# Alternating four and three seven-product pairs in the feed-forward slabs of a two-layer trunk, with the feed-forward cut into four groups

## The chip, the cores and the metric

The kernel runs on one core of a Trainium2 chip. Its engines work from queues of their own, each in order: TensorE (PE) multiplies matrices, VectorE (DVE) and ScalarE (ACT) work element by element, GpSimd (POOL) does little here, SyncE (SP) issues transfers. The metric is the time of one execution in microseconds on the device, median of several runs.

## What is computed

The reference is a trunk of two layers on 256 tokens of width 2048, in float32. The change lies in the second half of a layer:

```python
x = x + mix @ w_out[l]
h = _rmsnorm(x, norm2_g[l])
x = x + (jax.nn.silu(h @ ffn_w_gate[l]) * (h @ ffn_w_up[l])) @ ffn_w_down[l]
```

The hidden width D_FF is 5632, which is 44 blocks of 128 columns. The width 2048 is 16 chunks of 128. Ahead of this stand the input projection, eight retention heads and a gated recurrence; a final norm follows the second layer.

## The kernel before, in words

All weights come from memory in float32 and are split on the core into two parts, `whi` (ScalarE rounds a copy) and `wlo` (VectorE subtracts that copy from the weight), and every activation likewise into a pair (`op`). A product then takes three matmuls: high by high, high by low, low by high (L616 to L618). The down projection and the other projections with weights as the stationary side do the same with two matmuls a block, one of 512 and one of 256 columns (L233, L236).

The feed-forward of a layer is worked in groups (THIRDS), each of several slabs and then a down phase. A **slab** is four blocks of the hidden width (SLAB), gate and up together, for both halves of the tokens; a layer has 11 slabs, the groups of before 4, 4 and 3. A slab runs through the 16 chunks in eight pairs, one **unit** each. There are two kinds of unit:

- A plain unit (P) makes eight block products, 24 matmuls. Its weights (1 MB) are prepared in two halves of 1024 columns: two `whi` and two `wlo`.
- A unit with seven products (F, `p < FAST`) forms sums and differences of blocks first, a Strassen-like scheme with 21 matmuls. Its weights are prepared in four steps (`gate_parts`, `up_parts`, `first_sums`, `second_sums`): three halves of 1024, one of 512, and three extra subtractions on VectorE in the raw buffer (L649, L654, L655). The `whi` of `first_sums` needs the result of L655. The matching sums of the activations are made once a layer by `combined`, in the output projection, and stay for all slabs.

The order of a slab's units is F P F P F P P P. After the last F `shared` takes four sums out of PSUM (L705 to L710); at the slab's end `gate` and `up` (L714 to L721) combine the rest, `columns` transposes the result on TensorE (L731), and `operands_of` makes pairs of it (L143, L144). These pieces are issued some ticks later, among the next unit's blocks: a tick is one block of a unit.

After the slabs of a group come 16 units of the **down phase**, one for each chunk of the output, each over the group's 16 or 12 blocks of the hidden width, and each ends with `residual` (L462, L463), which adds the PSUM result to x. `hold` moves the last blocks of the first units behind one another, so that the last slab's operands have time to become ready.

Three raw buffers (RAW) take the weights; the load of unit n + 3 is issued after the last preparation of unit n. Six tiles each of `whi` and `wlo` (HALVES) hold prepared halves: ahead of every block `prepare` issues up to two preparations, as long as the half six places back has been used. The pairs of activations share 32 tiles (`ops`).

Of the kernel before, what the change touches and what calls it, by code (L numbers as in the profile page):

```python
# [11 lines left out]
F32 = mybir.dt.float32  # L12
F32R = mybir.dt.float32r
# [10 lines left out]
NL = 8  # L24
CHUNK = 64
EPS = 1e-6
THIRDS = [(0, 16), (16, 16), (32, 12)]
SLAB = 4
FAST = 3
RAW = 3  # L30
HALVES = 6
WARM = 12
# [56 lines left out]
def trunk(ctx: ExitStack, tc, a, out):  # L89
# [375 lines left out]
    def after_residual(k, nxt, gains):  # L465

        accumulate("xa", X[:, k, :], k == 0)
        st[nxt, k] = pair(X[:, k, :], gains(k))
        if k == KD - 1:
            tk.after(2, lambda: sums([st["xa"]], D, "rs"))  # L470
            if nxt == "h1":
                tk.after(4, lambda: rows("rs"))
        if nxt == "h2" and k % 2 and k < 2 * FAST:
            tk.after(3, lambda: combined(k // 2, gains))

    def combined(p, gains):

        r = one_p.tile([P, 4, T], F32, tag="rot4", name="asum")
        for i in range(2):
            S.activation(out=r[:, i, :], in_=X[:, 2 * p + i, :], func=AF.Copy, scale=gains(2 * p + i))  # L480
        a11, a21, a12, a22 = (r[:, i, j * P : (j + 1) * P] for i in range(2) for j in range(2))
        f = r[:, 2:4, :].rearrange("p a (b t) -> p (a b) t", b=2)
        V.tensor_tensor(out=f[:, 0, :], in0=a21, in1=a22, op=ALU.add)
        V.tensor_tensor(out=f[:, 1, :], in0=f[:, 0, :], in1=a11, op=ALU.subtract)
        V.tensor_tensor(out=f[:, 2, :], in0=a11, in1=a21, op=ALU.subtract)
        V.tensor_tensor(out=f[:, 3, :], in0=a12, in1=f[:, 1, :], op=ALU.subtract)
        if p == 0:
            st["s01"] = one_p.tile([P, 2, 4, 2, P], F32R, tag="v", name="s01")
        if p == 2:
            st["s2"] = one_p.tile([P, 4, 2, P], F32R, tag="gy0", name="s2")  # L490
        t = st["s2"] if p == 2 else st["s01"][:, p]
        S.activation(out=t[:, :, 0, :], in_=f, func=AF.Copy)
        V.tensor_tensor(out=t[:, :, 1, :], in0=f, in1=t[:, :, 0, :].bitcast(F32), op=ALU.subtract)
        st["sums", p] = t

    def rotation():
        r = one_p.tile([P, 2, T], F32, tag="rotl", name="rotl")
# [48 lines left out]
    def layer_units(l):  # L546
        res = v_units(l)
        res[0].begin = lambda: tk.after(30, rotation)
        proj = lambda n, done, begin=None: column_unit(
            a["w_in"][l, n], KD, lambda k: st["h1", k], done, begin)  # L550
        heads = []
        for h in range(NH):
            q_done, k_done, g_done = head(l, h)
            heads += [proj(h, q_done), proj(8 + h, k_done), proj(16 + h, g_done)]
        heads[-4], heads[-3], heads[-2] = heads[-3], heads[-2], heads[-4]
        for n in range(NL):
            x_begin, x_done, y_done = lru(l, n)
            res += [proj(24 + n, x_done, x_begin), proj(32 + n, y_done)]
            for _ in range(REC_AFTER[n] if n < NL - 1 else len(heads)):
                res.append(heads.pop(0))  # L560


        order = [0, 1, 2, 3, 4, 5, 6] + list(range(8, 16)) + [7]
        for n in range(KD):
            def done(ps, n=n):
                residual(n, ps)
                after_residual(n, "h2", lambda k: col("g2", l * KD + k))
            res.append(column_unit(a["w_out"][l, n], KD, lambda k: st["mix", l, k], done, order=order))
        hold(res[-KD : -KD + 2])


        for t, (f0, nf) in enumerate(THIRDS):
            for f in range(f0, f0 + nf, SLAB):
                res += slab_units(l, f, f == f0)
            res[-1].done = columns_again
            first = len(res)
            for n in range(KD):
                def done(ps, n=n, t=t):
                    residual(n, ps)
                    if t == len(THIRDS) - 1:  # L580
                        if l + 1 < DEPTH:
                            after_residual(n, "h1", lambda k: col("g1", (l + 1) * KD + k))
                        else:
                            last(n)
                res.append(column_unit(a[f"w_down{t}"][l, n], nf, lambda k, f0=f0: st["act", f0 + k], done))
            hold(res[first : first + (2 if nf == 16 else 3)])
        return res


    def slab_units(l, f0, first):  # L590
# [3 lines left out]

        c = {}
        res = []

        def start():
            if first:
# [32 lines left out]
        def piece(t, k):  # L632
            return t.rearrange("p (f k w) -> p f k w", f=SLAB, k=2)[:, :, k, :]

        turns = [q for p in range(FAST) for q in (p, FAST + p)] + list(range(2 * FAST, KD // 2))
        for p in turns:
            u = Unit(loader(p))
            plain = p >= FAST
            if not plain:
                def gate_parts(u=u):  # L640
                    hi, lo = half_tiles(u, 0)
                    parts(hi, lo, u.raw[:, 0:1024])

                def up_parts(u=u):
                    hi, lo = half_tiles(u, 1)
                    flat = lambda t: t[:, 0:512].rearrange("p (f w) -> p f w", f=SLAB)
                    parts(flat(hi), flat(lo), piece(u.raw[:, 1024:2048], 1))
                    r = u.raw.rearrange("p (c f k w) -> p c f k w", c=2, f=SLAB, k=2)
                    V.tensor_tensor(out=r[:, :, :, 0, :], in0=r[:, 1].rearrange("p f k w -> p k f w"),  # L649
                                    in1=r[:, :, :, 0, :], op=ALU.subtract)  # L650

                def first_sums(u=u):
                    g, p_ = u.raw[:, 0:1024], u.raw[:, 1024:2048]
                    V.tensor_tensor(out=piece(p_, 1), in0=piece(p_, 1), in1=piece(g, 0), op=ALU.subtract)  # L654
                    V.tensor_tensor(out=piece(g, 1), in0=piece(g, 1), in1=piece(p_, 1), op=ALU.subtract)  # L655
                    hi, lo = half_tiles(u, 2)
                    parts(hi, lo, g)

                def second_sums(u=u):
                    hi, lo = half_tiles(u, 3)  # L660
                    parts(hi, lo, u.raw[:, 1024:2048])

                u.preps = [gate_parts, up_parts, first_sums, second_sums]

                def run(todo, p=p, u=u):
                    def go():
                        if p == 0 and todo[0] == 1:
                            start()
                        s = st["sums", p]
                        form = lambda i: (s[:, i, 0, :], s[:, i, 1, :])  # L670
                        x = {1: lambda: block_of(0, 2 * p), 2: lambda: block_of(0, 2 * p + 1),
                             4: lambda: block_of(1, 2 * p + 1), 3: lambda: form(3), 5: lambda: form(0),
                             6: lambda: form(1), 7: lambda: form(2)}
                        w = {1: (0, 0), 2: (0, 1), 5: (2, 0), 4: (2, 1), 7: (3, 0), 6: (3, 1)}
                        for i in todo:
                            if i == 3:
                                t = tuple(t[1][:, 0:512] for t in (u.hi, u.lo))
                            else:
                                h, k = w[i]
                                t = piece(u.hi[h], k), piece(u.lo[h], k)  # L680
                            product(i, x[i](), t, False, p == FAST - 1 and i in (1, 5, 6, 7))
                    return go

                for todo, frees in (((1, 2), [0]), ((3, 5), [1]), ((4, 7), [2]), ((6,), [3])):
                    u.add(run(todo), frees)
                if p == FAST - 1:
                    u.done = lambda: tk.after(1, shared)
            else:
                plain_halves(u, 2048)
                for j, side, i in ((0, 0, 2), (1, 0, 4), (0, 1, 3), (1, 1, 8)):  # L690
                    def go(j=j, side=side, i=i, p=p, u=u):
                        for k in range(2):
                            product(i, block_of(j, 2 * p + k), (piece(u.hi[side], k), piece(u.lo[side], k)),
                                    False, p == KD // 2 - 1 and k == 1)
                        if p == KD // 2 - 1:
                            tk.after(1, {2: lambda: gate(0), 4: lambda: gate(1), 3: lambda: up(0), 8: lambda: up(1)}[i])
                    u.add(go, [side] if j else [])
            res.append(u)
# [290 lines left out]
```

## Time and profile before

| | |
|---|---|
| median of 3 runs | 2216.33 us (2216.12 to 2218.39) |
| profiled execution | 2215.92 us, of it a span of 2214.2 us |
| TensorE clock granted over the span | 0.997 of full speed |
| busy, share of the span | PE 99%, PEld (weight load, overlaps) 84%, DVE 80%, ACT 55%, POOL 2% |
| read from memory | 418.77 MB, 190 GB/s over the span |

The median is what a changed kernel is compared with. The profiled execution is a single one, and durations come from it. Busy shares are means over stages that differ. A matmul's recorded duration is longer than the distance to the next one's start, since matmuls are pipelined; the distance is what counts.

### The profile page before, as it was taken

The numbers are of one execution on the slowest core, as the hardware profiler recorded it, in microseconds if no ns is written. First come the engines' busy times: TensorE is split into PE (matmuls) and PEld (weight loads), VectorE is DVE, ScalarE is ACT, GpSimd is POOL, SyncE is SP. The second block draws the span as 40 slices with busy tenths as digits, with TensorE's granted clock in tenths as the row PEclk, the third lists the DMA queues.
The fourth block names the chain that finished last, engine by engine and source line by source line (L and its number), as shares of the span: only waits on it lengthen the run. The fifth ranks groups of instructions, "written<-read, shape, count | busy, mean of one in ns | idle before, by whom it ended". The sixth has DMA issues, their size and how long they took to land.

```text
span 2214.2 us, 29756 instructions
## 1 busy us (share of the span) xinstructions
PE 2194.4 (99%) x11322; PEld 1861.3 (84%) x11322; DVE 1774.1 (80%) x2547; ACT 1211.5 (55%) x1620; POOL 47.5 (2%) x97
## 2 busy tenths in 40 slices
PE   9999999999999999999999999999999999999997
PEld 7888888888888888888888888888888887888886
DVE  7888887988678985888858889779886788758875
ACT  6667554655446553455646665546554455535553
POOL 0000000000000000000000000000000000000000
PEclk9999999999999999999999999999999999999998
DMA  8555454566556665555655554546665555655563
GB/s 298 182 196 186 163 182 168 190 201 230 191 169 198 198 209 198 189 178 190 212 189 192 172 201 163 179 162 199 220 209 190 172 189 190 223 186 179 173 210 113
DMA packets 224224, 422.81 MB, mean 191 GB/s; under 512 B 10192, under 2 KB 191056, under 8 KB 200016
## 3 DMA queue, kind: packets, MB, share of 16 engines
q1 hardware_dynamic: 220992, 413.96, 55.7%
q0 software_dynamic: 1792, 5.24, 0.7%
q8 instruction: 89, 1.46, 0.3%
q10 hardware_dynamic: 1296, 1.70, 0.2%
q14 instruction: 55, 0.45, 0.1%
HBM read 418.77 MB, written 2.10 MB: 190 GB/s over the span
## 4 chain that ended last, share of the span: by engine, by line
PE 62%; issue 34%; DVE 2%; ACT 1%; POOL 0%; DMA 0%; ACTq 0%; DVEq 0%; POOLq 0%
PE acc_ps L233 24%; PE acc_ps L236 12%; PE row_ps L616 6%; PE row_ps L618 6%; PE row_ps L617 6%; PE acc_ps L523 1%; PE acc_ps L525 1%; PE acc_ps L524 1%; DVE wlo L206 1%; PE sm_ps L385 1%; PE sm_ps L731 1%; ACT whi L205 0%; PE sm_ps L294 0%; DMA x<-in_x_dram 0%; POOL rc L167 0%
## 5 line engine op out<-in xcount | busy, mean ns | idle before, releaser
L205 ACT ACTIVATE whi<-raw 128x1024 fp32r<-128x1024 f32 (+2 forms) x940 | 916.7, 1003 | 837.9 <-PE acc_ps L233 440.5
L206 DVE TENSOR_TENSOR wlo<-raw,whi 128x1024 fp32r<-128x1024 f32 (+2 forms) x940 | 1063.9, 1155 | 283.4 <-ACT whi L205 277.5
L233 PE MATMUL acc_ps<-op,whi 128*128 128x512 f32 x3200 | 1014.0, 398 | 0.0
L236 PEld LDWEIGHTS acc_ps<-op,wlo 128*128 128x128 f32 x3200 | 600.7, 188 | 140.8
L236 PE MATMUL acc_ps<-op,wlo 128*128 128x256 f32 x3200 | 630.2, 278 | 0.0
L233 PEld LDWEIGHTS acc_ps<-op,whi 128*128 128x128 f32 x3200 | 490.0, 189 | 1.6
L617 PE MATMUL row_ps<-wlo,op 128*128 128x512 f32 x1078 | 420.9, 390 | 0.0
L616 PE MATMUL row_ps<-whi,op 128*128 128x512 f32 x1078 | 420.1, 390 | 0.0
L618 PE MATMUL row_ps<-whi,op 128*128 128x512 f32 x1078 | 419.9, 390 | 0.0
L616 PEld LDWEIGHTS row_ps<-whi,op 128*128 128x128 f32 x1078 | 202.3, 188 | 42.2
L618 PEld LDWEIGHTS row_ps<-whi,op 128*128 128x128 f32 x1078 | 202.4, 188 | 41.9
L617 PEld LDWEIGHTS row_ps<-wlo,op 128*128 128x128 f32 x1078 | 202.4, 188 | 41.6
L462 DVE TENSOR_TENSOR x<-acc_ps,x 128x256 f32<-128x256 f32 x128 | 54.1, 422 | 77.6 <-PE acc_ps L236 77.4
L618 PE MATMUL row_ps<-whi,s 128*128 128x512 f32 x264 | 104.8, 397 | 0.0
L617 PE MATMUL row_ps<-wlo,s 128*128 128x512 f32 x264 | 104.5, 396 | 0.0
L616 PE MATMUL row_ps<-whi,s 128*128 128x512 f32 x264 | 103.5, 392 | 0.0
L649 DVE TENSOR_TENSOR raw<-raw 128x1024 f32<-128x1024 f32 x66 | 80.3, 1216 | 0.1
L143 ACT ACTIVATE op<-sm_ps 128x256 fp32r<-128x256 f32 x88 | 33.6, 381 | 72.0 <-DVE op L144 37.3
L618 PEld LDWEIGHTS row_ps<-whi,s 128*128 128x128 f32 x264 | 50.1, 190 | 9.7
L617 PEld LDWEIGHTS row_ps<-wlo,s 128*128 128x128 f32 x264 | 49.6, 188 | 10.3
L616 PEld LDWEIGHTS row_ps<-whi,s 128*128 128x128 f32 x264 | 49.6, 188 | 10.2
L463 DVE TENSOR_TENSOR x<-acc_ps,x 128x256 f32<-128x256 f32 x128 | 54.0, 422 | 3.2
(153 smaller groups left out, 1401.8 us busy)
## 6 DMA issues: line engine op xcount, KB each, us to landing
raw<-in_w_gate_dram SPq DMA_DIRECT2D x176, 512.0 KB, 3.6
raw<-in_w_up_dram SPq DMA_DIRECT2D x176, 512.0 KB, 5.3
raw<-in_w_in_dram SPq DMA_DIRECT2D x80, 1024.0 KB, 5.0
raw<-in_w_down_dram SPq DMA_DIRECT2D x64, 1024.0 KB, 5.0
raw<-in_w_out_dram SPq DMA_DIRECT2D x32, 1024.0 KB, 4.9
raw<-in_w_down_dram SPq DMA_DIRECT2D x32, 768.0 KB, 4.2
raw<-in_w_v_dram SPq DMA_DIRECT2D x12, 1024.0 KB, 5.0
raw<-in_w_v_dram SPq DMA_DIRECT2D x16, 256.0 KB, 5.9
```

The source lines that it names most:

```text
L143: S.activation(out=t[:, 0, :], in_=x_ap, func=AF.Copy)
L205: S.activation(out=hi, in_=raw, func=AF.Copy)
L206: V.tensor_tensor(out=lo, in0=raw, in1=hi.bitcast(F32), op=ALU.subtract)
L233: PE.matmul(u.ps, lhsT=u.hi[side(k)][:, col_of(k)], rhs=operand(k).rearrange("p a t -> p (a t)"), start=k == order[0], stop=False)
L236: PE.matmul(u.ps[:, T : 2 * T], lhsT=u.lo[side(k)][:, col_of(k)], rhs=operand(k)[:, 0, :], start=False, stop=k == order[-1])
L385: PE.matmul(ps[:, j * T : (j + 1) * T], lhsT=c["w"][:, j, :], rhs=c["xc"], start=True, stop=True)
L462: V.tensor_tensor(out=X[:, k, :], in0=ps[:, T : 2 * T], in1=X[:, k, :], op=ALU.add)
L463: V.tensor_tensor(out=X[:, k, :], in0=ps[:, 0:T], in1=X[:, k, :], op=ALU.add)
L616: PE.matmul(ps, lhsT=x[0], rhs=w[0], start=go, stop=False)
L617: PE.matmul(ps, lhsT=x[0], rhs=w[1], start=False, stop=False)
L618: PE.matmul(ps, lhsT=x[1], rhs=w[0], start=False, stop=end)
L649: V.tensor_tensor(out=r[:, :, :, 0, :], in0=r[:, 1].rearrange("p f k w -> p k f w"), in1=r[:, :, :, 0, :], op=ALU.subtract)
```

## The change

Slabs with an even number within the layer have four F units, in the order F P F F P F P P; the odd ones keep three. Each of a layer's six slabs with four has 180 matmuls in place of 183. `combined` is called for a fourth pair of chunks, and its sums are held in two tiles of `ops`. So that these and the group's operands fit into the 32 tiles, the groups of the feed-forward are made smaller: three of 12 blocks (three slabs each) and one of 8 (two slabs). Each layer then has four down phases of 16 units, and `hold` takes the first three units of a group of 12 and the first four of the group of 8.

```diff
-THIRDS = [(0, 16), (16, 16), (32, 12)]
+THIRDS = [(0, 12), (12, 12), (24, 12), (36, 8)]
-FAST = 3
+FAST = (4, 3)
...
-        if nxt == "h2" and k % 2 and k < 2 * FAST:
+        if nxt == "h2" and k % 2 and k < 2 * max(FAST):
             tk.after(3, lambda: combined(k // 2, gains))
...
+        if p < 3:
+            t = st["s2"] if p == 2 else st["s01"][:, p]
+            S.activation(out=t[:, :, 0, :], in_=f, func=AF.Copy)
+            V.tensor_tensor(out=t[:, :, 1, :], in0=f, in1=t[:, :, 0, :].bitcast(F32), op=ALU.subtract)
+            st["sums", p] = [t[:, i] for i in range(4)]
+        else:
+            st["sums", p] = []
+            for i in (0, 2):
+                t = op_p.tile([P, 2, T], F32R, tag="op", name="op").rearrange("p i (a t) -> p i a t", a=2)
+                S.activation(out=t[:, :, 0, :], in_=f[:, i : i + 2, :], func=AF.Copy)
+                V.tensor_tensor(out=t[:, :, 1, :], in0=f[:, i : i + 2, :], in1=t[:, :, 0, :].bitcast(F32), op=ALU.subtract)
+                st["sums", p] += [t[:, 0], t[:, 1]]
...
-            hold(res[first : first + (2 if nf == 16 else 3)])
+            hold(res[first : first + (3 if nf == 12 else 4)])
...
+        fast = FAST[f0 // SLAB % 2]
...
-        turns = [q for p in range(FAST) for q in (p, FAST + p)] + list(range(2 * FAST, KD // 2))
+        turns = {3: (0, 3, 1, 4, 2, 5, 6, 7), 4: (0, 4, 1, 2, 5, 3, 6, 7)}[fast]
...
-            plain = p >= FAST
+            plain = p >= fast
...
-                if p == FAST - 1:
+                if p == fast - 1:
                     u.done = lambda: tk.after(1, shared)
```

## Rows read from the trace of the kernel before

**Rows 1.** The page, busy time, share and instructions of each engine.

```profile
PE 2194.4 (99%) x11322; PEld 1861.3 (84%) x11322; DVE 1774.1 (80%) x2547; ACT 1211.5 (55%) x1620; POOL 47.5 (2%) x97
```

**Rows 2.** Windows: first, middle slab; down phase; last slab; down phase.

```profile
core 0: us, PE busy (x) PEld busy (x) DVE busy (x) ACT busy (x) POOL busy (x), PEclk, DMA share, GB/s
647.70:689.30 41.60, 41.60 (x185) 34.37 (x184) 36.37 (x40) 23.36 (x26) 0.00 (x0) 1.00 0.61 198
...
731.90:774.70 42.80, 42.80 (x192) 34.93 (x192) 38.61 (x46) 24.43 (x30) 0.00 (x0) 1.00 0.60 196
...
817.50:907.60 90.10, 90.10 (x522) 78.60 (x521) 56.88 (x73) 34.83 (x36) 0.00 (x0) 1.00 0.53 178
991.80:1034.70 42.90, 42.82 (x192) 34.93 (x191) 36.12 (x44) 24.00 (x30) 0.00 (x0) 1.00 0.60 208
1034.70:1101.60 66.90, 66.90 (x387) 58.31 (x386) 54.07 (x96) 39.43 (x65) 0.00 (x0) 1.00 0.58 193
```

**Rows 3.** Timeline of VectorE over one slab; brackets: idle before, releaser.

```profile
start us, us, engine line op out<-in xcount [idle before <-releaser]
727.27 2.36 DVE L206 TENSOR_TENSOR wlo<-raw,whi 128x1024 fp32r<-128x1024 f32 x2 [1.21 <-ACT whi L205]
...
742.56 6.37 DVE L206 TENSOR_TENSOR wlo<-raw,whi 128x1024 fp32r<-128x1024 f32 x6 [1.19 <-ACT whi L205]
...
752.72 6.90 DVE L206 TENSOR_TENSOR wlo<-raw,whi 128x1024 fp32r<-128x1024 f32 x6 [1.21 <-ACT whi L205]
...
770.10 2.36 DVE L206 TENSOR_TENSOR wlo<-raw,whi 128x1024 fp32r<-128x1024 f32 x2 [1.21 <-ACT whi L205]
...
775.91 0.74 DVE L721 SCALAR_TENSOR_TENSOR cb<-cb,rc,ca 128x512 f32<-128x512 f32 x1
```

**Rows 4.** Timeline of TensorE over the same slab (durations overlap, starts count).

```profile
731.94 0.39 PE L616 MATMUL row_ps<-whi,op 128*128 128x512 f32 x1
...
733.87 0.33 PE L731 MATMUL sm_ps<-ident,cb 128*128 128x128 f32 x1
...
743.36 0.39 PE L616 MATMUL row_ps<-whi,op 128*128 128x512 f32 x1
...
745.40 0.39 PE L616 MATMUL row_ps<-whi,s 128*128 128x512 f32 x1
...
748.12 0.39 PE L616 MATMUL row_ps<-whi,op 128*128 128x512 f32 x1
...
774.74 0.39 PE L616 MATMUL row_ps<-whi,op 128*128 128x512 f32 x1
```

**Rows 5.** Timeline of VectorE across the end of a group's last slab.

```profile
1030.38 0.96 DVE L206 TENSOR_TENSOR wlo<-raw,whi 128x768 fp32r<-128x768 f32 x1 [1.76 <-ACT whi L205]
...
1042.40 0.42 DVE L144 TENSOR_TENSOR op<-sm_ps,op 128x256 fp32r<-128x256 f32 x1
```

**Rows 6.** Waits over the span: us in total, times, longest us.

```profile
ACT whi L205 <- DVE raw L655: 229.5, 66, 4.8
```

**Rows 7.** VectorE instructions by line and form: count, busy, mean ns.

```profile
L206 DVE TENSOR_TENSOR wlo<-raw,whi 128x768 fp32r<-128x768 f32 x64 | 61.1, 955 | 24.8 <-ACT whi L205 24.1
L206 DVE TENSOR_TENSOR wlo<-raw,whi 128x512 fp32r<-128x512 f32 x82 | 55.8, 683 | 0.8 <-ACT whi L205 0.7
...
L462 DVE TENSOR_TENSOR x<-acc_ps,x 128x256 f32<-128x256 f32 x128 | 54.1, 422 | 77.6 <-PE acc_ps L236 77.4
...
L144 DVE TENSOR_TENSOR op<-sm_ps,op 128x256 fp32r<-128x256 f32 x88 | 36.5, 418 | 7.5 <-ACT op L143 7.5
...
L707 DVE TENSOR_TENSOR cb<-row_ps,ca 128x512 f32<-128x512 f32 x22 | 15.0, 684 | 0.0
...
L493 DVE TENSOR_TENSOR s<-asum,s 128x512 fp32r<-128x512 f32 x6 | 4.1, 689 | 2.8 <-ACT s L492 2.8
```

**Rows 8.** The page, transfers: KB of each, median us from issue to landing.

```profile
raw<-in_w_gate_dram SPq DMA_DIRECT2D x176, 512.0 KB, 3.6
raw<-in_w_up_dram SPq DMA_DIRECT2D x176, 512.0 KB, 5.3
```

More of the change, by code (lines that the diff above doesn't have):

```diff
@@ L490, in combined @@
             st["s2"] = one_p.tile([P, 4, 2, P], F32R, tag="gy0", name="s2")
[L491 to L494, printed above, removed]
+        if p < 3:
[10 more added lines that the diff above has]
+                st["sums", p] += [t[:, 0], t[:, 1]]
     def rotation():
@@ L669, in go @@
                         s = st["sums", p]
-                        form = lambda i: (s[:, i, 0, :], s[:, i, 1, :])
+                        form = lambda i: (s[i][:, 0, :], s[i][:, 1, :])
                         x = {1: lambda: block_of(0, 2 * p), 2: lambda: block_of(0, 2 * p + 1),
@@ L680, in go @@
                                 t = piece(u.hi[h], k), piece(u.lo[h], k)
-                            product(i, x[i](), t, False, p == FAST - 1 and i in (1, 5, 6, 7))
+                            product(i, x[i](), t, False, p == fast - 1 and i in (1, 5, 6, 7))
                     return go
```

## The prediction

> **What bounds the kernel now.** I read the page first, then the windows by stage, then the timelines of VectorE and TensorE over one slab, then the waits. The page names TensorE: busy 99%, VectorE 80%, ScalarE 55% [rows 1]. A share over the whole span hides two regimes, and the windows part them. In a down phase (16 units of 16 blocks) VectorE is busy 56.88 of 90.10 us; in a slab in the middle of a group it is busy 38.61 of 42.80 [rows 2]. The timeline shows how little of the rest is free. The same instruction, the third wlo of the first F unit, starts at 727.27 and at 770.10, 42.83 us apart, and TensorE's first matmuls of the two slabs are 42.80 apart [rows 3, 4]. So both engines have the same period. In that period VectorE has three gaps of about 1.2 us, one in each F unit; each stands ahead of a wlo that waits for ScalarE's whi, which itself waits for L655, and the waits count 66 of these, one for every F unit there is [rows 3, 6]. In-order queues on both engines force that gap. What is left free is about 0.5 us a slab. TensorE sets the end, and VectorE keeps up with it with nothing to spare.
>
> **The cost of one more F unit.** From the third wlo of one F unit to the third wlo of the next, with one P between, VectorE takes 752.72 - 742.56 = 10.16 us [rows 3]. A P unit is two wlo; six in a row span 6.90 us, so they follow each other after (6.90 - 1.22) / 5 = 1.136 us, and P takes 2.27 us. F takes 10.16 - 2.27 = 7.89 us, its 1.2 us gap included. On TensorE, F runs from 743.36 to 748.12, 4.76 us for 21 matmuls, 0.227 us each [rows 4]; P has 24 of these, 5.44 us. Turning a P into an F therefore takes 0.68 us from TensorE and puts 5.62 us on VectorE.
>
> **Part 1, TensorE's saving.** FAST alternates 4, 3 over the 11 slabs of a layer, so slabs 0, 2, 4, 6, 8 and 10 get one more F: 12 in the two layers. 12 x 3 x 0.227 = 8.2 us less.
>
> **Part 2, VectorE over a slab with four.** In the period of 42.83, three F and five P make 35.0; the rest, 7.4 and some 0.5 idle, is the combining at the end (eight instructions like L707, two L721 and four L144 [rows 7]). With four F and four P the sum is 31.6 + 9.1 + 7.4 = 48.1, against 42.8 - 0.7 = 42.1 on TensorE. I now follow where this 6.0 us comes out.
>
> *Two F in a row.* In the order F P F F P F P P the third F follows the second at once. Today the second F's third half is ready at 742.56 + 1.22 = 743.8, and TensorE asks for it at 745.40: 1.6 us to spare [rows 3, 4]. The next F's third half would be ready 7.89 later and wanted 4.76 later, so TensorE waits 7.89 - 4.76 - 1.6 = 1.55 us. The fourth F then comes 10.16 later on VectorE and 10.2 later on TensorE: no wait, nothing to spare. In the first slab of a group VectorE is 2.2 us less busy (36.37 against 38.61 [rows 2]), so there the wait lies between 0 and 1.55; I take 0.8. Slabs 0 and 6 of each layer are such: 4 x 0.8 + 8 x 1.55 = 15.6 us.
>
> *The slab behind it.* VectorE's queue holds, behind the last F, the P units, the combining, the next slab's first F, and then L720 and L721, for which TensorE's transposes wait. Today from the last F's third wlo (752.72) to the next slab's first L721 (775.91 + 0.74) it takes 23.9 us. With one P fewer in the tail it is 21.7 (23.9 - 2.27). Counting on from 742.56, the two F in a row and F P F put that third wlo at 742.56 + 7.89 + 10.16 = 760.6, so L721 ends at 782.3. TensorE, 0.68 shorter and 1.55 delayed, ends the slab at 774.74 + 0.87 = 775.6 and today's transposes start 733.87 - 731.94 = 1.9 later [rows 4], at 777.5. They come 4.8 us late; I take off 0.2, part of the slab's 0.5 of idle time: 4.6. TensorE works in order, so everything behind the transposes moves; after this delay VectorE stands to it as today. With the new groups of 3, 3, 3 and 2 slabs, the fast slabs 0, 4 and 6 of each layer are followed by a slab: 6 x 4.6 = 27.6 us.
>
> *The group's end.* Slabs 2, 8 and 10 are followed by a down phase. There VectorE prepares halves of 768 (0.955 us) or 512 (0.683) in place of an F [rows 7]: today the last slab of the third group has it busy 36.12 us, 2.5 less than a middle one [rows 2], and idle for 1.76 us ahead of a single half [rows 5]. The 4.6 us of lateness meets about as much cover. I take 0.3 us a time (bounds 0 and 2): 6 x 0.3 = 1.8.
>
> *Transfers.* Three raw buffers go round, so the load for the next slab's first unit starts with the last wlo of the fourth F, at 760.6 + 2.27 = 762.9. Its gate part lands 3.6 us later [rows 8] and its whi takes about as long as a wlo: 767.7, where VectorE would have come to it at 760.6 + 6 x 1.136 = 767.4. I take 0.3 us (bounds 0 and 1, the up part being 5.3 us behind its issue): 6 x 0.3 = 1.8 us.
>
> **Part 3, four groups.** The matmuls of the down phases stay the same (44 blocks for each of 16 columns; 90.1 / 256 = 0.352 us a block [rows 2]). Added are 32 units, with 32 x 2 evacuations of 0.42 us (L462 and its neighbour [rows 7]), 27 us of VectorE. In a down phase of 12 blocks VectorE needs 16 x (2 x 0.955 + 2 x 0.42), 44 us, in 67: hidden, and were there no cover it would cost those 27. In the last group a unit has 8 blocks, 2.8 us of TensorE; today's last phase has VectorE busy 54.07 / 16 = 3.4 a unit [rows 2], less 2 x 0.27 for smaller halves: 2.85. The two are level; I take 1.0 us in all (bounds 0 and 3). At the head of that group only four blocks, 5.6 us, and 0.9 of transposes stand ahead of the held ones, in place of six. The last operand is there today at 1042.40 + 0.42, 8.1 after the slab's end at 1034.7 [rows 2, 5]; the held block wants it at 5.6 + 0.9 + 0.7 = 7.2: 0.9 us, twice, 1.8. The fourth combined() adds a few instructions like L493 [rows 7] in the output projection, where VectorE has time: nothing, or 2 us a layer uncovered.
>
> **The sum.** -8.2 + 15.6 + 27.6 + 1.8 + 1.8 + 1.0 + 1.8 = +41.4. The profiled execution took 2215.9 us (a span of 2214.2 and 1.7 around it), 0.4 under the median of 2216.3. 2215.9 + 41.4 = 2257.3, by the median 2257.7; I say 2257.
>
> **Rivals.**
> *The look-ahead absorbs it (faster).* Six prepared halves are allowed, the third and fourth P give VectorE time, and the whole-span share is 80%. If VectorE found 5.6 us for each extra F, only TensorE's 8.2 would count, with 2.8 for the last group: 2210.5. It decides at a free time of 5.6 us in a slab; the rows show 0.5, or 4.1 with all three 1.2 us gaps filled, and none of them is. Chance 0.05, a fifth of it close enough to be called no change.
> The Trainium skill ("Perfetto Trace Analysis", Identifying the Most-Contended Engine) says that the engine with the highest occupancy is the most contended and should be optimized first. By that rule over the whole span (99% against 80%) the change would pay all of its saving: 2215.9 - 8.2 = 2207.7 us. The slab windows, VectorE busy 38.61 of 42.80 with its forced gaps on top, do not bear the rule out for these stages.
>
> *Another order on the queues.* When VectorE is late, L714, L720 and L721 may be placed in the gap of the next F, or the transposes behind more matmuls. That would give back up to 1.2 and 1.6 us six times: 2257 - 17 = 2240. Today's trace shows L144 next to such a gap but not in it. Chance 0.14.
>
> *VectorE sets every fast slab, group ends too.* Then each of 12 costs 48.1 - 42.8 = 5.3: 2215.9 + 63.6 + 2.8 = 2282. Against it speaks the idle time at the group's end [rows 5]. Chance 0.08.
>
> **How the numbers follow.** My case has 0.73, and by its own bounds (0 to 1.55 in four first slabs, 0 to 2 at six ends, 0 to 1 six times, 0 to 3) it spans 2249 to 2271. With the next two cases taken in as far as needed the range is 2240 to 2274. About 0.2% (4.4 us) is what a measurement can tell from no change. Faster 0.04, same 0.02, slower 0.94.
>
> **What will show it.** Right: a slab with four of about 43 us and the slab behind it near 47; in the waits L731 on DVE L721 grows from under 2 us to 4 or 5 a time in six places; a wait of 1.5 us on a wlo at the third F; 1330 x 3 matmuls of L616 to L618 at an unchanged 0.227; VectorE close to gapless but for the 1.2 us gaps over pairs of slabs, down phases as they were but for the head of the last. Wrong: if VectorE's gaps after L655 are filled, or its wlo run ahead by more than today at the head of the slab behind a fast one, the price goes with them.

## The result

| | us, median of runs | ratio to before, 95% interval |
|---|---|---|
| before | 2216.2 (2216.0 to 2218.4) | |
| after | 2240.5 (2238.1 to 2243.6) | 1.0106 (1.0094 to 1.0118) |

The change makes the kernel slower, by 24.3 us. 41 were forecast, in a range of 2240 to 2274: the direction and the engine were right, and the size was not; the result lies at the lower edge of the range (the ratio times the 2216.33 of before gives 2239.8). The profiled execution of after took 2238.1 us, 22.1 more than that of before (2215.9), and the rows below are from it.

### The profile page after: what moved, and what is told of

Its sections match the earlier page's. It is cut to its first block, busy times and chain, and to the rows that moved or that the text cites. A ratio compares the mean times of both kernels' runs of the same rounds, so it can differ in the third digit from the quotient of the medians.

```text
span 2236.3 us, 30194 instructions
## 1 busy us (share of the span) xinstructions
PE 2200.4 (98%) x11286; PEld 1852.6 (83%) x11286; DVE 1852.5 (83%) x2747; ACT 1237.3 (55%) x1716; POOL 47.3 (2%) x97
## 4 chain that ended last, share of the span: by engine, by line
PE 55%; issue 35%; DVE 6%; DMA 2%; ACT 2%; POOL 0%; ACTq 0%; SPq 0%; DVEq 0%; POOLq 0%
PE acc_ps L233 24%; PE acc_ps L236 12%; PE row_ps L626 4%; PE row_ps L627 4%; PE row_ps L625 4%; DVE wlo L206 3%; ACT whi L205 1%; PE acc_ps L531 1%; PE acc_ps L533 1%; PE acc_ps L532 1%; PE sm_ps L385 1%; DMA raw<-in_w_gate_dram 1%; DMA raw<-in_w_down_dram 0%; DMA raw<-in_w_up_dram 0%; PE sm_ps L741 0%
## 5 line engine op out<-in xcount | busy, mean ns | idle before, releaser
L205 ACT ACTIVATE whi<-raw 128x1024 fp32r<-128x1024 f32 (+2 forms) x1028 | 942.2, 948 | 816.8 <-PE acc_ps L233 430.0
L206 DVE TENSOR_TENSOR wlo<-raw,whi 128x1024 fp32r<-128x1024 f32 (+2 forms) x1028 | 1092.3, 1089 | 239.4 <-ACT whi L205 234.4
L625 PE MATMUL row_ps<-whi,op 128*128 128x512 f32 x1066 | 412.6, 391 | 5.1 <-DVE op L144 4.0
L627 PE MATMUL row_ps<-whi,op 128*128 128x512 f32 x1066 | 415.7, 391 | 0.0
L462 DVE TENSOR_TENSOR x<-acc_ps,x 128x256 f32<-128x256 f32 x160 | 67.6, 422 | 63.8 <-PE acc_ps L236 63.8
L659 DVE TENSOR_TENSOR raw<-raw 128x1024 f32<-128x1024 f32 x78 | 95.2, 1220 | 0.2
L463 DVE TENSOR_TENSOR x<-acc_ps,x 128x256 f32<-128x256 f32 x160 | 67.6, 423 | 3.6
```

The costliest lines, as they stand in the source:

```text
L205: S.activation(out=hi, in_=raw, func=AF.Copy)
L206: V.tensor_tensor(out=lo, in0=raw, in1=hi.bitcast(F32), op=ALU.subtract)
L462: V.tensor_tensor(out=X[:, k, :], in0=ps[:, T : 2 * T], in1=X[:, k, :], op=ALU.add)
L463: V.tensor_tensor(out=X[:, k, :], in0=ps[:, 0:T], in1=X[:, k, :], op=ALU.add)
L625: PE.matmul(ps, lhsT=x[0], rhs=w[0], start=go, stop=False)
L627: PE.matmul(ps, lhsT=x[1], rhs=w[0], start=False, stop=end)
```

## The profile after

The page's first part, as in [rows 1]:

```profile
PE 2200.4 (98%) x11286; PEld 1852.6 (83%) x11286; DVE 1852.5 (83%) x2747; ACT 1237.3 (55%) x1716; POOL 47.3 (2%) x97
```

VectorE is busy 78 us more, TensorE's share falls from 99% to 98%. The windows, to be held against [rows 2]: slabs 2, 4 and 8 have four F units, slab 5 is the slab behind slab 4; then comes a down phase of 12 blocks.

```profile
core 0: us, PE busy (x) PEld busy (x) DVE busy (x) ACT busy (x) POOL busy (x), PEclk, DMA share, GB/s
...
474.40:521.70 47.30, 44.80 (x190) 35.22 (x189) 43.13 (x52) 26.81 (x35) 0.00 (x0) 0.96 0.59 193
631.00:674.00 43.00, 42.66 (x190) 34.19 (x188) 38.70 (x47) 23.15 (x29) 0.00 (x0) 1.00 0.57 184
674.00:718.50 44.50, 43.44 (x192) 34.69 (x191) 39.72 (x47) 25.96 (x34) 0.00 (x0) 1.00 0.62 205
718.50:786.40 67.90, 67.90 (x393) 59.20 (x392) 48.02 (x73) 28.96 (x36) 0.00 (x0) 1.00 0.54 176
871.80:916.20 44.40, 42.74 (x190) 34.03 (x188) 39.43 (x47) 24.65 (x32) 0.00 (x0) 1.00 0.58 190
```

Slab 4 takes 43.0 us, as forecast ("about 43"), but the slab behind it 44.5 and not "near 47". VectorE over these two slabs, from the third wlo of one F to that of the next (columns: start, duration, line, count, idle time ahead in brackets; after's L665 is before's L655, L717 to L731 are L707 to L721):

```profile
641.48 4.10 DVE L206 TENSOR_TENSOR wlo<-raw,whi 128x1024 fp32r<-128x1024 f32 x4 [1.19 <-ACT whi L205]
...
649.38 6.37 DVE L206 TENSOR_TENSOR wlo<-raw,whi 128x1024 fp32r<-128x1024 f32 x6 [1.21 <-ACT whi L205]
...
659.54 6.90 DVE L206 TENSOR_TENSOR wlo<-raw,whi 128x1024 fp32r<-128x1024 f32 x6 [1.21 <-ACT whi L205]
...
669.62 0.68 DVE L717 TENSOR_TENSOR cb<-row_ps,ca 128x512 f32<-128x512 f32 x1
...
671.42 0.68 DVE L665 TENSOR_TENSOR raw<-raw 128x512 f32<-128x512 f32 x1
...
672.62 0.69 DVE L724 TENSOR_TENSOR ca<-row_ps,ca 128x512 f32<-128x512 f32 x1
673.22 0.68 DVE L720 TENSOR_TENSOR ca<-ca,cb 128x512 f32<-128x512 f32 x1
673.82 2.36 DVE L206 TENSOR_TENSOR wlo<-raw,whi 128x1024 fp32r<-128x1024 f32 x2
...
679.01 0.75 DVE L731 SCALAR_TENSOR_TENSOR cb<-cb,rc,ca 128x512 f32<-128x512 f32 x1
```

From 641.48 to 649.38 are 7.90 us for an F behind an F and from there to 659.54 are 10.16 for F and P, where the forecast had 7.89 and 10.16. The tail is different. The combining (L717 on) and the first of the two additions at the slab's end (L724) now stand between and behind the next slab's subtractions, and the third wlo at 673.82 starts with no gap ahead of it. In [rows 3] the same place, 770.10, had its 1.21 us. Here is TensorE at the third F and at the head of the slab behind, and ScalarE at the same F:

```profile
647.04 0.39 PE L625 MATMUL row_ps<-whi,op 128*128 128x512 f32 x1
...
649.40 0.50 PE L625 MATMUL row_ps<-whi,s 128*128 128x512 f32 x1
...
650.34 0.73 PE L625 MATMUL row_ps<-whi,s 128*128 128x512 f32 x2 [0.22 <-ACT whi L205]
650.91 0.39 PE L626 MATMUL row_ps<-wlo,s 128*128 128x512 f32 x1
...
652.78 0.39 PE L627 MATMUL row_ps<-whi,s 128*128 128x512 f32 x1
...
674.00 0.39 PE L625 MATMUL row_ps<-whi,op 128*128 128x512 f32 x1
...
679.96 0.27 PE L741 MATMUL sm_ps<-ident,cb 128*128 128x128 f32 x1
...
686.86 0.47 PE L625 MATMUL row_ps<-whi,op 128*128 128x512 f32 x1 [0.81 <-DVE op L144]
...
689.46 0.73 PE L625 MATMUL row_ps<-whi,s 128*128 128x512 f32 x2 [0.22 <-ACT whi L205]
```

```profile
648.28 5.37 ACT L205 ACTIVATE whi<-raw 128x1024 fp32r<-128x1024 f32 x6 [4.42 <-DVE raw L665]
```

The third half of the F that begins at 647.04 is wanted nine matmuls later, at 649.08. Its whi is ready at 648.28 + 1.06 = 649.34 (one such whi takes 1.06 us), its wlo at 649.38 + 1.22 = 650.60. TensorE does not wait for the wlo: from 649.40 it makes the four products that need only whi, of this half and the next, and takes up wlo at 650.91. The matmul at 652.78 is the unit's last; one matmul of the next unit stands among its own, so it is the 22nd, and it starts 652.78 - 647.04 = 5.74 us after the first. 21 distances took 4.76 in [rows 4], so 0.98 us are lost; 1.55 were forecast. In the slab behind, the transposes stand 5.96 us from the slab's first matmul (674.00 to 679.96), where it was 1.93 [rows 4], with other matmuls moved ahead of them; TensorE runs up to them without a wait. At 686.86 a matmul comes 0.81 us late, and at the third half of this slab's second F the pattern of 649.40 comes back, with another 0.8 us lost by 689.80. The waits (us in total, times, longest), to be held against [rows 6]:

```profile
ACT whi L205 <- DVE raw L665: 180.7, 53, 4.9
...
PEld row_ps L625 <- ACT whi L205: 23.4, 31, 2.0
...
PE row_ps L625 <- ACT whi L205: 9.6, 20, 1.6
...
PEld sm_ps L741 <- DVE cb L731: 5.5, 10, 1.4
...
PE row_ps L625 <- DVE op L144: 4.0, 6, 0.8
...
PE sm_ps L741 <- DVE cb L731: 2.7, 5, 1.2
```

ScalarE waits for the last subtraction 53 times, and there are 78 F units. That is not yet a count of VectorE's gaps: at 659.54 the gap is there and ScalarE was released by a matmul. Counted in VectorE's timeline, 56 of the 78 F have the full gap, 16 a shorter one with one or two instructions in it, and six, at the heads of the slabs behind a slab with four, none; in the kernel before 62 of 66 had the full one. The forecast wait of 4 to 5 us a time on `cb` L731 is not there: all waits of the transposes for it make 8.2 us in 15 pieces, and before it was 8.8 in 16. A wait that the prediction did not have is: six times, once in each slab behind a slab with four, a matmul waits for L144. The code says why: `columns` puts its transposes into the one PSUM bank that product 8 uses too, so the first P unit's last block can start only when the second L144 pair has read the bank. Transposes moved back by 4 us move that too.

## The experiments

**Theory A**: VectorE's time sets the price; an extra F is 5.6 us more on an engine with nothing free. **Theory B**: it is the order; where two F follow each other prepared halves run out, whatever VectorE's total. **Theory C**: the four groups, with a short last phase and 32 more evacuations.

**The groups alone.**

```diff
-FAST = (4, 3)
+FAST = (3, 3)
```

> The four groups with every slab at three F units. Theory A (VectorE's time in the slabs with four sets the price): the regrouping costs only what the down phases showed, 3 to 5 us less a little at fewer slab ends: 2216 to 2222 us. Theory C (the new groups, their short last phase and more evacuations are the price): 2232 to 2241 us.

Measured: 2217.05 us beside 2217.42 of before, ratio 0.9997 (0.9988 to 1.0006). The regrouping costs nothing that can be measured, and theory C falls. In the profiles, by TensorE's starts, two effects cancel: all that lies outside the slabs is 3.6 us longer than before, and the slabs together are 2.3 us shorter, since each layer has one more first slab (41.58 us in place of 42.63).

**No two F in a row.**

```diff
-        turns = {3: (0, 3, 1, 4, 2, 5, 6, 7), 4: (0, 4, 1, 2, 5, 3, 6, 7)}[fast]
+        turns = {3: (0, 3, 1, 4, 2, 5, 6, 7), 4: (0, 4, 1, 5, 2, 6, 3, 7)}[fast]
```

> The slabs with four in the order F P F P F P F P, so that no F follows an F inside a slab. Theory A: VectorE has the same work, so 2234 to 2248 us, the wait only moving from the third F to the head of the next slab. Theory B (two F in a row run out of prepared halves; the order is the price): the wait goes, 2212 to 2224 us.

Measured: 2224.73 us, ratio 1.0034 (1.0022 to 1.0046), some 16 us better than the change. Theory A alone, as expected from it, is refuted: the same work on VectorE costs much less in another order. B is not enough either, since the kernel stays 7 us slower than before although TensorE has 8 us less to do. Windows of this kernel, slabs 4 and 5:

```profile
627.30:669.20 41.90, 41.90 (x189) 34.32 (x188) 37.88 (x46) 22.30 (x29) 0.00 (x0) 1.00 0.57 187
669.20:714.70 45.50, 43.96 (x192) 34.73 (x191) 40.50 (x48) 26.61 (x34) 0.00 (x0) 1.00 0.60 201
```

The slab with four now takes 41.9 us, all of TensorE's saving; the price, 2.9 us, stands in the slab behind.

**The fourth F without its three subtractions** (this leaves them out for `p == 3`, so these products are of other numbers):

```diff
...
+                    if p == 3:
+                        return
...
+                    if p != 3:
+                        V.tensor_tensor(out=piece(p_, 1), in0=piece(p_, 1), in1=piece(g, 0), op=ALU.subtract)
+                        V.tensor_tensor(out=piece(g, 1), in0=piece(g, 1), in1=piece(p_, 1), op=ALU.subtract)
```

> Leaves out the three subtractions in the raw buffer for the fourth F unit of the slabs with four, so its products are of other numbers; matmuls, order, groups and transfers stay. Theory A: 12 times 2.6 us of VectorE and 1.2 us of gap go, 46 us; what is left of an extra F is under 2 us, so nearly the whole price goes: 2212 to 2221 us. Theory B: the pair of F in a row is untouched, 2228 to 2238 us.

Measured: 2220.61 us, ratio 1.0014 (1.0005 to 1.0023). VectorE is busy 26 us less than in the change (1852.5 to 1826.1), and the 12 gaps go as well; that takes 20 us off, although the pair of F in a row is still there. So VectorE's time in the slab, gap included, is most of the price, and the pair's own part remains: slab 4 of this kernel takes 42.8.

**Filler on VectorE in the kernel before.** The first of two tries:

```diff
...
+                if p == FAST and f0 // SLAB % 2 == 0:
+                    def filled(then=u.preps[1]):
+                        then()
+                        for _ in range(16):
+                            V.tensor_tensor(out=idle, in0=idle, in1=idle, op=ALU.max)
+                    u.preps[1] = filled
```

> The kernel before with 16 idle VectorE instructions of 256 columns (about 0.34 us apart, 5.5 us) behind the first P unit's preparation in every slab of even number; nothing else is changed, three F each, the old groups. Theory A: VectorE's 5.5 us more in 12 slabs have the effect of the fourth F, 2238 to 2262 us. Theories B and C: VectorE is busy 80% and has room, 2215 to 2222 us.

Measured: 2227.25 us, ratio 1.0044 (1.0030 to 1.0058), which tells nothing of the slabs. The filler depends on nothing, and in the program built it ran ahead of them (line of the tile `idle`: count, duration, first and last start):

```profile
L695 DVE TENSOR_TENSOR idle<-idle x192: 376/418/503, 1.3 to 357.3; 128x256 f32<-128x256 f32 x192
```

All 192 have started by 357.3 us, before the first slab, and 9.2 of the 10 us lie ahead of it (its first matmul starts at 396.8 in place of 387.5). What it does show is that the order of a queue is not that of the source: here instructions that depend on nothing stand far ahead of the code around them. The second try reads the raw buffer of its unit, behind the third F:

```diff
-                if p == FAST and f0 // SLAB % 2 == 0:
+                if p == FAST + 2 and f0 // SLAB % 2 == 0:
-                    def filled(then=u.preps[1]):
+                    def filled(then=u.preps[1], u=u):
...
-                            V.tensor_tensor(out=idle, in0=idle, in1=idle, op=ALU.max)
+                            V.tensor_tensor(out=idle, in0=u.raw[:, 1792:2048], in1=u.raw[:, 1024:1280], op=ALU.max)
```

> The filler once more, now reading the raw buffer of the unit behind the third F, so that it can only run in its slab: 16 instructions of 256 columns, 5.5 us of VectorE, in the slabs of even number of the kernel before. Theory A (VectorE's time in the slab is the price, less what falls into the gaps behind the last subtraction and under the group's end): the changed kernel lost about 31 us to waits for 12 times 5.6 us, so 20 to 33 us here too, 2236 to 2250 us. Theory B (not the time, but the place of two F in a row): no F follows an F here, 2216 to 2224 us.

Measured: 2233.56 us, ratio 1.0072 (1.0055 to 1.0088): 16 us for 66 us of VectorE, with three F and none behind another. That is less than A expected and more than B. Work on VectorE costs, but not all of it:

```profile
ACT whi L206 <- DVE raw L656: 155.1, 46, 6.6
...
ACT whi L206 <- DMA raw<-in_w_gate_dram: 39.7, 34, 2.8
```

46 waits in place of 66, and in VectorE's timeline the full gap stands in only 32 of the 66 F units: other instructions have been put into the rest, whose idle time falls from 77 to 51 us in all. The gaps which I had called forced are forced only for the work around them in the kernel before. The test is not clean, though. The filler holds its raw buffer for longer, so later loads start later: ScalarE waits 39.7 us for the gate weights, where it was 9.6 in 19 pieces before. How much of the 16 us is VectorE's time and how much the loads is not parted.

**Filling the gap on purpose.** In both kernels the sum that is complete one subtraction earlier is split first:

```diff
-                    parts(hi, lo, g)
+                    parts(hi, lo, p_)
...
-                    parts(hi, lo, u.raw[:, 1024:2048])
+                    parts(hi, lo, u.raw[:, 0:1024])
...
-                        w = {1: (0, 0), 2: (0, 1), 5: (2, 0), 4: (2, 1), 7: (3, 0), 6: (3, 1)}
+                        w = {1: (0, 0), 2: (0, 1), 7: (2, 0), 6: (2, 1), 5: (3, 0), 4: (3, 1)}
...
-                for todo, frees in (((1, 2), [0]), ((3, 5), [1]), ((4, 7), [2]), ((6,), [3])):
+                for todo, frees in (((1, 2), [0]), ((3, 7), [1]), ((6, 5), [2]), ((4,), [3])):
```

In the changed kernel:

> The changed kernel with the two prepared sums of an F unit in the other order: the half that is complete one subtraction earlier is split first, so that ScalarE rounds it while VectorE makes the last subtraction, and TensorE takes the products in that order (1 2, 3 7, 6 5, 4). The gap in each F on VectorE should fall from 1.2 to about 0.5 us. Theory A: VectorE per F 7.2 in place of 7.9 us, a pair of slabs 86 us against 84 on TensorE, so 2212 to 2224 us. Theory B: the halves still come too late at the second of two F, 2230 to 2240 us.

In the kernel before:

> The same order of the sums in the kernel before. Theory A: TensorE is the bound there and VectorE only just keeps up, so little can be won: 2208 to 2216 us. Theory B: no effect, 2215 to 2218 us.

Measured: 2214.66 us, ratio 0.9984 (0.9975 to 0.9993), in the changed kernel and 2212.15 us, 0.9976 (0.9967 to 0.9985), in the kernel before. The gap falls as expected (VectorE of the kernel before with this order, from the last subtraction on):

```profile
749.88 0.69 DVE L655 TENSOR_TENSOR raw<-raw 128x512 f32<-128x512 f32 x1
751.05 2.36 DVE L206 TENSOR_TENSOR wlo<-raw,whi 128x1024 fp32r<-128x1024 f32 x2 [0.48 <-ACT whi L205]
```

0.7 us less on VectorE in each F gives the changed kernel 26 us back. Two F in a row then cost nothing: its slab 4, still with the pair, takes 41.9 us, so it was the late halves that cost and not the order as such. The kernel before wins 5; its slabs no longer stretch (42.6 us each, where six had taken 42.8 to 42.9 and two 43.8 and 43.9). Theory A's numbers hold here.

**The combining one tick earlier.**

```diff
-                    u.done = lambda: tk.after(1, shared)
+                    u.done = lambda: shared()
```

> The changed kernel with the combining behind the last F issued one tick earlier. In the order built from it the four instructions stand between the P units' wlo and the first ca/cb additions fill the gap of the next slab's first F. If VectorE's total is what counts (A), 2234 to 2243 us, as with the change; if the combining's place in the gap is what made the slab behind cheaper than predicted, and is lost, up to 2247 us.

Measured: 2238.94 us, ratio 1.0100 (1.0085 to 1.0114), as the change. The gap at the head of the slab behind is then filled by other instructions; the place of these four does not matter to the time.

**Both orders together** (the diffs of the alternating order and of the sums):

> Both: the other order of the sums, and F P F P F P F P in the slabs with four. Theory A with the order's part added: VectorE's gaps are 0.5 us and no F follows an F, so the slabs with four take 41.9 us, the ones behind them 42.6: TensorE's 8.2 us saved against the kernel before with that order of the sums (2212.2), 2204 to 2209 us, faster than all so far. If the slabs behind still wait for VectorE, 2210 to 2214 us.

Measured: 2214.11 us, ratio 0.9987 (0.9978 to 0.9996), against 2204 to 2209 expected of theory A; it is the other case, slabs behind that still wait. The slabs with four in the middle of a group take 41.9 us, and the slabs behind still 44.0. From the waits of the whole run:

```profile
PE row_ps L625 <- DVE op L144: 4.8, 6, 0.8
...
PEld sm_ps L741 <- DVE cb L731: 3.1, 9, 0.8
```

The six waits of 0.8 us for the bank that transposes and product 8 share stand one in each slab behind. In slab 5 this is the only stop of TensorE's matmuls longer than 0.1 us, and with its restart it makes 1.0 of the 1.3 us above 42.6.

**Four F only where no slab follows**, in the last slab of each group, 8 in all:

```diff
-        fast = FAST[f0 // SLAB % 2]
+        fast = 4 if f0 + SLAB in [g + n for g, n in THIRDS] else 3
```

with the alternating order, then with the order of the sums as well, then in the change's order with two F in a row:

> The order F P F P F P F P, with four F only in the last slab of each group (8 slabs), where the down phase follows; the sums in the change's order. If the lateness is absorbed at the group's end, these slabs cost 41.95 us in place of 42.6 and nothing behind them: 8 times 0.7 us gained on the four groups with three F (2217), 2210 to 2213 us. If VectorE's 5.6 us have to be paid there too, 2225 us and more.

> Four F only in the last slab of each group, order F P F P F P F P, and the other order of the sums (the last subtraction under ScalarE's rounding). Theory A with the order's part: the two gains add, since the first takes matmuls from TensorE and the second the stretching of the middle slabs: 2210.4 less 3 to 5, 2205 to 2208 us. If VectorE is no longer late anywhere, the order of the sums brings nothing on top: 2209 to 2211 us.

> As the kernel with four F only in the last slab of each group, but in the change's order F P F F P F P P. If the pair of F in a row costs what the slabs behind a slab with three show (42.95 us against 41.95), 8 times 1.0 us: 2217 to 2220 us. If the order costs only where a slab follows, 2210 to 2213 us.

Measured: 2210.37 us, ratio 0.9969 (0.9957 to 0.9980); 2208.76 us, 0.9967 (0.9954 to 0.9979); 2219.58 us, 1.0015 (1.0006 to 1.0024). Windows of the first of these three kernels, a middle slab with three F and the last slab of its group with four:

```profile
623.90:666.50 42.60, 42.60 (x192) 34.91 (x192) 38.37 (x45) 24.32 (x30) 0.00 (x0) 1.00 0.59 191
666.60:708.70 42.10, 42.07 (x189) 34.32 (x188) 38.05 (x46) 24.08 (x31) 0.00 (x0) 1.00 0.58 195
```

At a group's end the fourth F is paid for by the down phase's spare time, as the prediction had it: these slabs take 41.95 to 42.24 us, so VectorE's 5.6 us cost 0.3 us at most, and TensorE keeps its saving. The two F in a row cost (2219.6 - 2210.4) / 8 = 1.15 us each. The first two kernels beat before and after; between them the runs do not decide, and the second lies between its two expected ranges, so the sums' order, worth 5 us in the kernel before, brings little on top.

## Why the prediction was right or wrong

Slab lengths from TensorE's starts (first matmul of a slab to that of what follows), in us; slabs of the first layer, and in bold those with four F:

| slab | place | three F, new groups | after | alternating order |
|---|---|---|---|---|
| 1 | behind slab 0 | 42.54 | 45.27 | 46.40 |
| 2 | end, behind slab 1 | 42.63 | **47.23** | **42.50** |
| 4 | middle | 42.63 | **42.97** | **41.95** |
| 5 | end, behind slab 4 | 43.29 | 44.53 | 45.51 |
| 6 | first | 41.58 | **41.55** | **40.90** |
| 7 | behind slab 6 | 42.63 | 43.85 | 44.77 |
| 8 | end, behind slab 7 | 43.03 | **44.37** | **42.34** |
| 10 | end, behind slab 9 | 42.63 | **42.97** | **41.95** |

I hold the lengths of after, both layers, against 42.63 (first slabs 41.58, the layers' first 42.09, slab 1 42.54), less 0.68 where there are four F.

*TensorE's saving, -8.2.* Right. 1066 + 264 groups of three matmuls in place of 1078 + 264, still 0.227 us apart.

*VectorE's cost, 7.89 and 10.16 us.* Right, as measured above.

*Two F in a row, 15.6.* Too large: about 0.7 us in each of four first slabs and 1.0 in the eight others, 10.7 in all (the 1.0 is measured in slabs 4 and 10 and taken over for 2 and 8, which carry more than the pair). The step "TensorE waits 7.89 - 4.76 - 1.6 = 1.55" compared the end of the half's wlo with the first matmul that uses the half. That matmul needs whi alone, and the matmuls with whi of two halves were placed ahead.

*The slab behind it, 27.6.* This is the step that failed most: "at 777.5 ... They come 4.8 us late" and "after this delay VectorE stands to it as today". The slabs behind lost 11.7 us (2.7 and 2.9, twice 1.9, 1.2 and 1.1), and the fast slabs behind these another 9.0 above the 1.0 for their pair: 20.7 in all. The 4.6 did not stand at the transposes, which the new program has 4 us further back, and the 1.2 us gap at the slab's head was filled. The lateness is carried along instead: in slab 5 about 1 us of it comes out at product 8's bank and 0.8 at the third half of the next F; part comes out in the next slab with four; and what is left at the group's end costs next to nothing, 1.3 and 0.3 us in the two down phases behind slab 8. The rival "another order on the queues" is what happened; I gave it 0.14. That its 2240 us was met as well is partly luck: of the 18 us by which the sum was too large, 8.7 (with the 1.8 for transfers) lie here, and the rest at the pair and in the terms for the group's end and the new groups. I had counted with today's order of VectorE's queue, when the change itself sets a new one. The sign stood in the trace of before, in another slab than the one I read; I had written that L144 stands next to such a gap but not in it:

```profile
437.65 0.68 DVE L655 TENSOR_TENSOR raw<-raw 128x512 f32<-128x512 f32 x1
438.25 0.42 DVE L144 TENSOR_TENSOR op<-sm_ps,op 128x256 fp32r<-128x256 f32 x1
439.52 6.37 DVE L206 TENSOR_TENSOR wlo<-raw,whi 128x1024 fp32r<-128x1024 f32 x6 [0.85 <-ACT whi L205]
```

*Transfers, 1.8.* Not seen: ScalarE's waits for gate and up weights are 14.5 us in all, and were 20.7 before.

*The group's end and the new groups, 1.8 + 1.0 + 1.8.* The group's end cost about 1.6 us in place of 1.8. For the new groups the 2.8 is not far off what lies outside the slabs, 3.6, but the slabs' own gain of 2.3 was left out; together regrouping measured -0.4 us, within its interval of about 2 us either way. The fourth `combined`, put at nothing, shows nothing: the first slab starts at 387.1 us, before at 387.5.

Together -8.2 + 10.7 + 20.7 = +23.2, beside 24.3 in the medians and 22.1 in the profiles. The closeness is partly luck too, since these lengths are held against undisturbed ones. Straight from the profiles, the 22 slabs went from 936.2 to 953.6 us, +17.4, and all the rest from 1277.9 to 1282.7, +4.7: the slabs of before already lost 3.6 us, and regrouping saves 2.1 by two more first slabs.

*The rivals.* That the look-ahead absorbs it did not happen, nor that VectorE sets every fast slab. The 2207.7 us that the prediction drew from the rule of the Trainium skill ("Perfetto Trace Analysis", Identifying the Most-Contended Engine) did not come either: VectorE's share of the span, 80% before, was no room in the slabs. For TensorE the same section sets the matmuls' busy share aside and judges by the share of the peak rate and by the weight load's busy share; the latter was 84% before, so the order of the two engines stays.

*The range.* The bounds named in the prediction add up to 2249 and 2277, not 2271.

Left open: how much of the slab behind is the shared bank's. Its waits stand in the trace (4.0 us in after, 4.8 with both orders), but no kernel with another bank was tried, and none with more tiles for prepared halves.

## What to carry to other kernels

An engine with a low share of the span may still have no time left in one stage; compare its period with the bounding engine's period there, gaps included. Put extra work of such an engine into the last stage before one where it is idle. In the alternating order the fourth F cost 8 us in every other slab and gained 7 in the groups' last slabs; in the order of the change it cost 23 and 3 (all beside 2217 us for the same groups with three F). Before you count a gap as forced, ask what else can be put there, and which operand the next matmul really needs first; the order of an in-order queue is a result of the change, not a given.

## What was not expected

TensorE's clock dipped once within the profile of after. In slab 2 the third F waited 1.54 and 0.22 us for whi, and then the granted clock was 0.50, the lower of its two levels, for some 3 us (1.2 GHz; columns as in the windows above):

```profile
495.00:496.00 1.00, 0.37 (x2) 0.30 (x2) 0.39 (x1) 1.00 (x2) 0.00 (x0) 1.00 0.00 0
496.00:497.00 1.00, 0.78 (x3) 0.40 (x2) 1.00 (x2) 1.00 (x2) 0.00 (x0) 0.86 0.00 0
497.00:498.00 1.00, 1.00 (x4) 0.74 (x3) 1.00 (x2) 1.00 (x2) 0.00 (x0) 0.50 0.00 0
498.00:499.00 1.00, 1.00 (x4) 0.80 (x3) 1.00 (x1) 1.00 (x2) 0.00 (x0) 0.50 0.00 0
...
500.00:501.00 1.00, 1.00 (x5) 0.80 (x4) 1.00 (x2) 0.00 (x0) 0.00 (x0) 0.93 1.06 365
```

Matmuls stood 0.43 us apart there in place of 0.23 (498.34, 498.77, 499.19 by the timeline). Slab 2 took 47.2 us and the same slab of the second layer, with a full clock, 45.0. That is some 2 us of the 9.0 above. The wait alone does not decide it: slab 2 of the second layer waits 1.56 us at the same place and shows no dip, and with the combining one tick earlier the same two places waited as long and the dip came in the second layer only, where the slab took 46.4 us and the first layer's 44.6. So two of four such waits were followed by a dip, and each time the slab was about 2 us longer; why these two is not shown.
